# A hybrid attention block: the low part of the queries in zero-padded 128-row tiles

## The chip, the cores and the metric

The kernel runs on one core of one Trainium2 chip. The metric is device time in microseconds from start to end of one launch. TensorE (PE) multiplies, VectorE (DVE), ScalarE (ACT) and GpSimd (POOL) do the elementwise work, and SyncE (SP) issues the DMAs. A number like L413 is line 413 of the kernel before; the changed kernel's lines stand a few higher.

## The reference

One transformer block on 1024 tokens of width 1024, all in float32. A normalised input is projected into two attentions. The first (8 heads of 64) mixes three dilated windows, which is one softmax with a table of log multiplicities. The second (8 heads in 2 groups, one key head per group) has three branches: compressed keys, the 8 best blocks of 64 keys, and a window of 512. Their outputs are gated and summed, both attentions are normalised and projected, and a feed-forward layer with squared ReLU follows.

```python
s = jnp.einsum('bhrnqd,bhrnkd->bhrnqk', qs, kb) * (hd ** -0.5)      # dilated
sc = jnp.einsum('bgrqd,bgcd->bgrqc', qb, k_cmp) * scale             # compressed keys
p_cmp = masked_softmax(sc, cmp_end[None, :] <= tpos[:, None])
imp = jnp.einsum('bgrqc,cs->bgqs', p_cmp, overlap)                  # ranks the blocks
ss = jnp.einsum('bgrqd,bgqkd->bgrqk', qb, kg) * scale               # selected blocks
sw = jnp.einsum('bgrqd,bgkd->bgrqk', qb, kw) * scale                # window
out = gb[..., 0:1] * o_cmp + gb[..., 1:2] * o_sel + gb[..., 2:3] * o_win
h_res = h_res + mixed @ w_out[l]
h_res = h_res + jnp.square(jax.nn.relu(h @ w_up[l])) @ w_down[l]
```

## The kernel before

Float32 products are made from numbers split in two: a high part in the rounded format fp32r and a low part, the rest. A projection or MLP product is three matmuls: high x high, high x low, low x high (L334 to L336 for the projections, L709 to L711 for out_proj, L1021 to L1023 and L1055 to L1057 for the MLP).

Scores use that a head has only 64 rows. `k_stacks` and `q_stacks` turn 128-token tiles over on PE (L359) and stack two halves into 128 rows. For an even head (or group 0) the key stack holds the high keys in rows 0 to 63 and the low keys in rows 64 to 127; for an odd head (or group 1) it is the other way round. The query stack has the high queries in both halves. So one 128-row pass (L411) gives high x high + high x low. The low queries lie in a tile `q2`: rows 0 to 63 those of the even head, rows 64 to 127 those of the odd one. A second pass (L413) takes the 64 rows of the head and the same 64 rows of the key stack, which are its high keys, and adds low x high to the same bank. The queries are the stationary operand, up to 512 key columns the moving one. A unit is one head of one 128-query tile; more than 4 key blocks are cut in two chunks. Each chunk takes one of three score banks `S`.

The rest of a unit: DVE adds a table (window, multiplicity or block mask) and takes the extreme (L422), ACT exponentiates (L427), ACT, DVE and POOL split the result into two float16 parts (L441, L443, L445), a DMA on SP's queue transposes them into `pt` (L446), and PE multiplies them with the values (L461, L462). In the sparse attention the diagonal block of a selected branch gets its causal mask by a matmul with an identity (L415).

For the compressed keys of a 128-query tile (L754 to L758), each of four head pairs gets a 128-column pass of `q2` against `kch` (the high keys of group 0 and group 1, zeros elsewhere, so that all 128 rows of `q2` serve both groups), a mask by an identity matmul, and one 64-column pass per group of the query stack against `kcs`.

The stages in time: normalisation and the first projections to about 70 us; dilated attention of four head pairs between the other projections (scores from 71 to 337 us); the last projections; sparse attention over eight query tiles in the order 5, 7, 6, 4, 3, 2, 1, 0, between which out_proj is pushed in pieces (scores from 372 to 724 us); and the MLP from about 760 us to the end. The order on each engine is set by a scheduler in the compiler from priorities and its own cost model. The projections have a lower priority than the attention, so they fill in.

`cst`, `asp`, `bqp` and `bpp` are memory pools. `asp` lives through the dilated attention; `bqp` and `bpp` hold what the sparse attention needs, `bpp` from when the projection's memory is free. A query tile of the sparse attention is loaded from DRAM into `qr` (`q_load`, L734) and stacked (`q_build`) a tile ahead of its use. Names in the profile: `S`, `T`, `F`, `O` are banks (scores, transposes, products, outputs), `aq` and `ak` the stacks of the dilated attention, `qb` and `kb` those of the sparse one.

Of the kernel before, what the change touches and what calls it, by code (L numbers as in the profile page):

```python
# [9 lines left out]
F32 = mybir.dt.float32  # L10
# [27 lines left out]
FB = "qr qb qb2 ot cs cm oc".split()  # L38
# [7 lines left out]
CM = 1  # L46
# [10 lines left out]
def build(tc, A, out):  # L57
# [315 lines left out]
    def q_stacks(qe, qo, q2, srcs):  # L373
        n = len(srcs)
        ps = transposes(srcs)
        for e, o, i in zip(QS, (qe[0:64], qo[64:128], qe[64:128], qo[0:64]), (0, 64, 0, 64)):
            if e == "A":
                act.activation(o, ps[i:i + 64, :n], AF.Copy, scale=0.125)
            else:
                dve.tensor_scalar(o, ps[i:i + 64, :n], 0.125, None, op0=OP.mult)  # L380
        dve.scalar_tensor_tensor(q2[0:64], ps[0:64, :n], 0.125, f32(qe[0:64]), op0=OP.mult, op1=OP.subtract)
        dve.scalar_tensor_tensor(q2[64:128], ps[64:128, :n], 0.125, f32(qo[64:128]), op0=OP.mult, op1=OP.subtract)
# [11 lines left out]
    def st_scores(u):  # L394
# [12 lines left out]
        for j, (a, b) in enumerate(cuts):  # L407
# [5 lines left out]
            u["lastQ"] = pe.matmul(ps[:, :w], u["q2"], u["k"][u["r"], cs], start=False, stop=not diag)  # L413
# [107 lines left out]
    kch = cst.tile([128, 2, 64], F32R, name="kch")  # L521
    dve.tensor_scalar(kch, ident.rearrange("p (a b) -> p a b", a=2), 0.0, None, op0=OP.mult)
# [8 lines left out]
    def compress(kind):  # L531
# [36 lines left out]
        if kind == 0:  # L568
# [13 lines left out]
            act.activation(kch[0:64, 0], ps[0:64, 0, 0:64], AF.Copy)  # L582
            act.activation(kch[64:128, 1], ps[0:64, 0, 64:128], AF.Copy)
# [11 lines left out]
    def a_pair(hp):  # L595
# [5 lines left out]
        for a in (4, 0):  # L601
# [3 lines left out]
            q2 = asp.tile([128, 4, 128], F32R, name="aq2", bufs=1)  # L605
# [9 lines left out]
            for i in range(3, -1, -1):  # L615
                for e in range(2):
                    r = slice(64 * e, 64 * e + 64)
                    u = dict(q=q[:, e, i], q2=q2[r, i], r=r, k=k[:, e].rearrange("p a b -> p (a b)"),
# [7 lines left out]
    la = asp.tile([128, T], F32, name="la")  # L626
    sp.dma_start(la, A["la"])
# [102 lines left out]
    fbn = {}  # L730

    def q_load(i):
        QR[i] = big("qr0")[:, :512] if i == ORD[0] and "qr" in FB else bpp.tile([128, 512], F32, name="qr", bufs=2)
        sp.dma_start(QR[i], qbd[i])  # L734

    def q_build(i):
        q = fb(i, [128, 2, 4, 128], F32R, "qb", 2)
        q2 = fb(i, [128, 4, 128], F32R, "qb2", 2)
# [3 lines left out]

    def rows(g):
        return slice(64 * g, 64 * g + 64)

    def cmp_stages(i):
        st = {}

        def c1():
# [3 lines left out]
            for j in range(4):  # L753
                pe.matmul(ps[:, j], q2[:, j], kch, start=True, stop=False)  # L754
                if CM:
                    pe.matmul(ps[:, j], identb, cmask[:, i, None, :].to_broadcast([128, 2, 64]), start=False, stop=False)
                for g in range(2):
                    pe.matmul(ps[:, j, g], q[:, g, j], kcs[:, g], start=False, stop=g == 1)  # L758
# [48 lines left out]
    def b_attend(i, br):  # L807
# [4 lines left out]
        def f(br, h):  # L812
# [6 lines left out]
            u = dict(i=i, h=h, q=q[:, g, j], q2=q2[rows(g), j], r=rows(g), k=k[:, a * 128:], n=n,  # L819
# [53 lines left out]
    for step in P0:  # L873
        if step == "X":
# [14 lines left out]
            addt = bqp.tile([128, NT, 16], F32, name="addt")  # L889
            sp.dma_start(ctmp[:, :512], A["cmask"].rearrange("p a b -> p (a b)"))  # L890
# [35 lines left out]
    bpp, bpp_close = mkpool("bpp", side="right")  # L926
    for tag in ("ns", "hl", "pt"):
        xtra[tag] = (bpp, 0)
# [287 lines left out]
```

## Time and profile before

| what | value |
|---|---|
| time, median of 3 runs | 1474.64 us (1473.95 to 1474.69) |
| profiled execution, span | 1473.5 us |
| mean granted TensorE clock | 0.973 |
| PE, DVE, ACT, POOL busy | 98%, 55%, 42%, 35% |

The profiled execution shows its span from the first to the last instruction, 1473.5 us; the median run is 1.1 us above it. In a group of instructions stand the line, engine, operation, the tiles written and read, the sizes, the count, then the busy time in us and the mean of one in ns, then the idle time before them and what ended it. A matmul's size such as 64\*128 is rows and columns of its stationary tile. PE's busy time is modelled, and its matmuls overlap in the records: a matmul's record ends after the next has started, so the distance from start to start tells what one costs. In the tables by stretch PEclk is the granted clock as a share of full speed.

### The profile page before, as it was taken

Reading aid. Unit: us, or ns where it says so; the run is one execution under the profiler, and the core shown is the slowest. Engines: PE = TensorE matmul, PEld = TensorE weight load, DVE = VectorE, ACT = ScalarE, POOL = GpSimd, SP = SyncE. Lnnn points to the kernel's source line nnn. Section 1 sums busy time; section 2 is a strip of 40 time slices with the busy share of each in tenths; the row PEclk is TensorE's granted clock in tenths of the full one; section 3 lists DMA queues with packets and bytes.
Section 4 is the critical chain, followed back from the end, with each engine's and each line's share of the span. In section 5 each row is a group of like instructions: output and inputs, shape, how many; then the busy total and the mean of one; then the engine's idle time right before and its main releaser. Section 6 shows DMA issues by size and latency. Waiting matters only on the chain.

```text
span 1473.5 us, 21774 instructions
## 1 busy us (share of the span) xinstructions
PE 1437.5 (98%) x8235; PEld 1158.6 (79%) x8235; DVE 804.7 (55%) x1723; ACT 621.9 (42%) x1094; POOL 512.4 (35%) x728
## 2 busy tenths in 40 slices
PE   8999999999999999999899999999999999999997
PEld 6879888889866677677677888888888888888886
DVE  6565655774457776777545444444444444444436
ACT  7462746753656766677545221121221121221115
POOL 3435553654455556666711111111111111111113
PEclk9999999999968999799899999999999999999999
DMA  5255472957556866567523111111111111111002
GB/s 187 59 106 137 89 152 66 204 129 168 94 147 141 147 132 124 127 120 120 94 76 100 58 50 49 31 51 50 57 54 47 29 55 46 58 56 45 1 1 114
DMA packets 285192, 131.53 MB, mean 89 GB/s; under 512 B 219040, under 2 KB 272288, under 8 KB 285088
## 3 DMA queue, kind: packets, MB, share of 16 engines
q1 hardware_dynamic: 284944, 129.90, 37.8%
q8 instruction: 64, 1.05, 0.3%
q14 instruction: 40, 0.33, 0.1%
q10 hardware_dynamic: 144, 0.26, 0.0%
HBM read 68.26 MB, written 8.39 MB: 52 GB/s over the span
## 4 chain that ended last, share of the span: by engine, by line
PE 89%; DMA 3%; DVE 2%; POOL 2%; issue 1%; ACT 1%; SPq 0%; POOLq 0%; DVEq 0%; ACTq 0%
PE dn L1055 8%; PE dn L1057 8%; PE dn L1056 8%; PE up L1023 8%; PE up L1021 7%; PE up L1022 7%; PE S L413 7%; PE S L411 5%; PE F L334 4%; PE F L335 4%; PE F L336 4%; PE O L461 3%; PE T L359 2%; PE F L709 2%; PE F L710 2%; PE F L711 2%
## 5 line engine op out<-in xcount | busy, mean ns | idle before, releaser
L1032 POOL TENSOR_TENSOR ul<-ua,uh 128x512 fp32r<-128x512 f32 x64 | 83.5, 1305 | 611.0 <-ACT uh L1031 531.8
L1058 DVE SCALAR_TENSOR_TENSOR st<-dn,r2q,st 128x512 f32<-128x512 f32 (+1 forms) x257 | 191.5, 746 | 157.4 <-PE dn L1057 153.9
L1055 PE MATMUL dn<-wdh,uh 128*128 128x512 f32 (+1 forms) x514 | 202.8, 395 | 0.0
L1057 PE MATMUL dn<-wdh,ul 128*128 128x512 f32 (+1 forms) x514 | 202.3, 394 | 0.0
L1056 PE MATMUL dn<-wdl,uh 128*128 128x512 f32 (+1 forms) x514 | 201.4, 392 | 0.0
L1021 PE MATMUL up<-h2h,wuh 128*128 128x512 f32 x480 | 188.3, 392 | 1.0 <-ACT wuh L94 1.0
L1023 PE MATMUL up<-h2h,wul 128*128 128x512 f32 x480 | 188.4, 393 | 0.5 <-DVE wul L95 0.5
L1022 PE MATMUL up<-h2l,wuh 128*128 128x512 f32 x480 | 187.7, 391 | 0.0
L334 PE MATMUL F<-wh,hh 128*128 128x256 f32 (+1 forms) x576 | 166.5, 290 | 2.5 <-DVE vt L213 1.5
L335 PE MATMUL F<-wl,hh 128*128 128x256 f32 (+1 forms) x576 | 165.9, 289 | 0.0
L336 PE MATMUL F<-wh,hl 128*128 128x256 f32 (+1 forms) x576 | 164.5, 286 | 0.0
L427 ACT ACTIVATE ns<-ns,mn 128x640 f32<-128x640 f32 (+7 forms) x152 | 110.5, 747 | 58.1 <-POOL mn L426 28.8
L1029 ACT ACTIVATE ua<-up 128x512 f32<-128x512 f32 x60 | 35.3, 588 | 232.6 <-PE up L1023 232.6
L443 POOL TENSOR_TENSOR hl<-ns,hl 128x640 f16<-128x640 f32 (+5 forms) x67 | 104.0, 1554 | 36.3 <-ACT hl L441 30.4
L1057 PEld LDWEIGHTS dn<-wdh,ul 128*128 128x128 f32 x514 | 96.7, 188 | 22.6
L1056 PEld LDWEIGHTS dn<-wdl,uh 128*128 128x128 f32 x514 | 96.7, 188 | 21.9
L334 PEld LDWEIGHTS F<-wh,hh 128*128 128x128 f32 x576 | 108.1, 188 | 7.3 <-issue 3.4
L1055 PEld LDWEIGHTS dn<-wdh,uh 128*128 128x128 f32 x514 | 96.8, 188 | 21.1
L95 DVE TENSOR_TENSOR wul<-wur,wuh 128x1024 fp32r<-128x1024 f32 x32 | 39.4, 1230 | 134.4 <-ACT wuh L94 134.4
L335 PEld LDWEIGHTS F<-wl,hh 128*128 128x128 f32 x576 | 108.5, 188 | 4.5 <-issue 3.4
L336 PEld LDWEIGHTS F<-wh,hl 128*128 128x128 f32 x576 | 108.4, 188 | 3.7 <-issue 3.2
L1023 PEld LDWEIGHTS up<-h2h,wul 128*128 128x128 f32 x480 | 90.6, 189 | 20.5 <-DVE wul L95 1.0
(262 smaller groups left out, 3002.3 us busy)
## 6 DMA issues: line engine op xcount, KB each, us to landing
wur<-in_w_up_dram SPq DMA_DIRECT2D x32, 512.0 KB, 4.2
wdr<-in_w_down_dram SPq DMA_DIRECT2D x32, 512.0 KB, 3.8
wr<-in_w_in_dram SPq DMA_DIRECT2D x44, 256.0 KB, 3.2
st<-in_x_dram SPq DMA_DIRECT2D x8, 512.0 KB, 6.1
wor<-in_w_out_dram SPq DMA_DIRECT2D x16, 256.0 KB, 3.2
ns<-in_xT_dram SPq DMA_DIRECT2D x7, 512.0 KB, 4.9
out_dram<-st SPq DMA_DIRECT2D x7, 512.0 KB, 2.6
w<-in_w_k_dram SPq DMA_DIRECT2D x4, 512.0 KB, 5.1
```

The lines of the kernel that those rows point to most:

```text
L334: pe.matmul(ps, hh[:, k, ts], hi, start=k == 0, stop=False)
L335: pe.matmul(ps, hh[:, k, ts], lo, start=False, stop=False)
L336: pe.matmul(ps, hl[:, k, ts], hi, start=False, stop=k == KD - 1)
L427: u["exp"] = act.activation(ns[:, :n * 128], ns[:, :n * 128], AF.Exp, scale=-1.0, bias=mn[:, j:j + 1])
L443: pool.tensor_sub(lo, p, hi)
L1021: pe.matmul(ps, hi[:, k], h2h[:, k, hs], start=k == 0, stop=False)
L1022: pe.matmul(ps, hi[:, k], h2l[:, k, hs], start=False, stop=False)
L1023: pe.matmul(ps, lo[:, k], h2h[:, k, hs], start=False, stop=k == KD - 1)
L1055: pe.matmul(ps, uh[:, ts], wh[:, cs], start=j == 0, stop=False)
L1056: pe.matmul(ps, uh[:, ts], wl[:, cs], start=False, stop=False)
L1057: pe.matmul(ps, ul[:, ts], wh[:, cs], start=False, stop=j == NB - 1)
L1058: dve.scalar_tensor_tensor(o[:, cs], ps, r2q[:, t:t + 1], o[:, cs], op0=OP.mult, op1=OP.add)
```

## The change

The low queries move into a tile with a place of its own for each of the two heads (or groups). Head 0's low queries stand in rows 0 to 63 of the first half, and rows 64 to 127 there are zero; head 1's stand in rows 64 to 127 of the second half, and rows 0 to 63 there are zero. The second score pass then takes all 128 rows of this tile and all 128 rows of the key stack; the zeros meet the low keys. Three such tiles are made once and kept: `aq2` for the dilated attention, and two that take turns in the sparse one. Their zero halves are written once by DVE when the tile is made, two passes of 64 x 512 each.

The compressed keys use the same tiles: the pass against `kch` is replaced by one 64-column pass per group against `kcs`, the mask comes first, and `kch` with its zero fill and its two ACT copies is gone. The three tiles take twice the memory; `kch` and one of two `qr` buffers are given up.

```diff
-FB = "qr qb qb2 ot cs cm oc".split()
+FB = "qr qb ot cs cm oc".split()
...
-        dve.scalar_tensor_tensor(q2[0:64], ps[0:64, :n], 0.125, f32(qe[0:64]), op0=OP.mult, op1=OP.subtract)
-        dve.scalar_tensor_tensor(q2[64:128], ps[64:128, :n], 0.125, f32(qo[64:128]), op0=OP.mult, op1=OP.subtract)
+        dve.scalar_tensor_tensor(q2[0:64, 0], ps[0:64, :n], 0.125, f32(qe[0:64]), op0=OP.mult, op1=OP.subtract)
+        dve.scalar_tensor_tensor(q2[64:128, 1], ps[64:128, :n], 0.125, f32(qo[64:128]), op0=OP.mult, op1=OP.subtract)
+
+    def q2_tile(p, name):
+        t = p.tile([128, 2, 4, 128], F32R, name=name, bufs=1)
+        for e, rs in ((0, slice(64, 128)), (1, slice(0, 64))):
+            dve.tensor_scalar(t[rs, e], ident[rs, None, :].to_broadcast([64, 4, 128]), 0.0, None, op0=OP.mult)
+        return t
...
-            u["lastQ"] = pe.matmul(ps[:, :w], u["q2"], u["k"][u["r"], cs], start=False, stop=not diag)
+            u["lastQ"] = pe.matmul(ps[:, :w], u["q2"], u["k"][:, cs], start=False, stop=not diag)
...
-    kch = cst.tile([128, 2, 64], F32R, name="kch")
-    dve.tensor_scalar(kch, ident.rearrange("p (a b) -> p a b", a=2), 0.0, None, op0=OP.mult)
...
-            act.activation(kch[0:64, 0], ps[0:64, 0, 0:64], AF.Copy)
-            act.activation(kch[64:128, 1], ps[0:64, 0, 64:128], AF.Copy)
...
-            q2 = asp.tile([128, 4, 128], F32R, name="aq2", bufs=1)
+            q2 = aq2
...
-                    u = dict(q=q[:, e, i], q2=q2[r, i], r=r, k=k[:, e].rearrange("p a b -> p (a b)"),
+                    u = dict(q=q[:, e, i], q2=q2[:, e, i], k=k[:, e].rearrange("p a b -> p (a b)"),
...
+    aq2 = q2_tile(asp, "aq2")
...
-        QR[i] = big("qr0")[:, :512] if i == ORD[0] and "qr" in FB else bpp.tile([128, 512], F32, name="qr", bufs=2)
+        QR[i] = big("qr0")[:, :512] if i == ORD[0] and "qr" in FB else bpp.tile([128, 512], F32, name="qr", bufs=1)
...
-        q2 = fb(i, [128, 4, 128], F32R, "qb2", 2)
+        q2 = Q2[ORD.index(i) % 2]
...
-                pe.matmul(ps[:, j], q2[:, j], kch, start=True, stop=False)
-                if CM:
-                    pe.matmul(ps[:, j], identb, cmask[:, i, None, :].to_broadcast([128, 2, 64]), start=False, stop=False)
+                pe.matmul(ps[:, j], identb, cmask[:, i, None, :].to_broadcast([128, 2, 64]), start=True, stop=False)
                 for g in range(2):
+                    pe.matmul(ps[:, j, g], q2[:, g, j], kcs[:, g], start=False, stop=False)
                     pe.matmul(ps[:, j, g], q[:, g, j], kcs[:, g], start=False, stop=g == 1)
...
-            u = dict(i=i, h=h, q=q[:, g, j], q2=q2[rows(g), j], r=rows(g), k=k[:, a * 128:], n=n,
+            u = dict(i=i, h=h, q=q[:, g, j], q2=q2[:, g, j], k=k[:, a * 128:], n=n,
...
+            Q2.append(q2_tile(bqp, "qb20"))
...
+    Q2.append(q2_tile(bpp, "qb21"))
```

The scheduler orders the changed program anew. Up to the last head pair of the dilated attention it stands nearly as before; in the sparse stage pieces of out_proj and of the products with the values change places with scores. Three places matter for the prediction.

On PE, the scores against the compressed keys of the second query tile in the sparse attention. Before:

```order
L411 MATMUL S<-kb,qb 128x256
L413 MATMUL S<-kb,qb_5515 128x256
L754 MATMUL S<-kch,qb_5894 128x2x64
L756 LDWEIGHTS identb
L756 MATMUL S<-cmask,identb 128x2x64
L758 MATMUL S<-kcs,qb_5893 128x64 x2
```

Now:

```order
L417 MATMUL S<-kb,qb 128x256
L419 MATMUL S<-kb,qb_5449 128x256
L754 LDWEIGHTS identb
L754 MATMUL S<-cmask,identb 128x2x64
L756 MATMUL S<-kcs,qb_4806 128x64
L757 MATMUL S<-kcs,qb_5896 128x64
L756 MATMUL S<-kcs,qb_4806 128x64
L757 MATMUL S<-kcs,qb_5896 128x64
```

The score pair stands as it stood (the listing gives the size of the output, not the rows of the stationary tile). A 128-column pass is gone and two of 64 columns are new.

On DVE, where the key stack of the selected branch is built (L370, L371), at the start of the sparse stage. Before:

```order
L213 TENSOR_SCALAR st<-F,rms 128x128
L213 TENSOR_SCALAR vt<-F,r1v 128x128
L836 TENSOR_SCALAR den<-ot_4853,vsc 128x8
L837 RECIPROCAL den<-den 128x8
L370 TENSOR_TENSOR kb_5452<-T,kb_5452 64x512
```

Now:

```order
L213 TENSOR_SCALAR st<-F,rms 128x128
L213 TENSOR_SCALAR vt<-F,r1v 128x128
L387 TENSOR_SCALAR qb_5449<-c_ident 64x512 x2
L835 TENSOR_SCALAR den<-ot_4846,vsc 128x8
L836 RECIPROCAL den<-den 128x8
L370 TENSOR_TENSOR kb_5452<-T,kb_5452 64x512
```

The zero fill of the second sparse tile now stands three instructions ahead of that stack.

On SP's queue, the query loads. Before:

```order
L734 DMA qr<-qbd 128x512 x2
L682 DMA st<-in_x_dram 128x1024 x2
L734 DMA qr<-qbd 128x512
L656 DMA wor<-in_w_out_dram 128x512
L681 DMA oat<-oad 128x512
```

Now:

```order
L737 DMA qr<-qbd 128x512
L684 DMA st<-in_x_dram 128x1024 x2
L737 DMA qr<-qbd 128x512
L658 DMA wor<-in_w_out_dram 128x512
L683 DMA oat<-oad 128x512
```

The places are the same, and each holds the load of one tile earlier than before.

More of the change, by code (lines that the diff above doesn't have):

```diff
@@ L616, in a_pair @@
                 for e in range(2):
-                    r = slice(64 * e, 64 * e + 64)
-                    u = dict(q=q[:, e, i], q2=q2[r, i], r=r, k=k[:, e].rearrange("p a b -> p (a b)"),
+                    u = dict(q=q[:, e, i], q2=q2[:, e, i], k=k[:, e].rearrange("p a b -> p (a b)"),
                              n=a + i + 1, tab=la[:, (7 - a - i) * 128:],
@@ L730, in build @@
     fbn = {}
+    Q2 = []
     def q_load(i):
-        QR[i] = big("qr0")[:, :512] if i == ORD[0] and "qr" in FB else bpp.tile([128, 512], F32, name="qr", bufs=2)
+        QR[i] = big("qr0")[:, :512] if i == ORD[0] and "qr" in FB else bpp.tile([128, 512], F32, name="qr", bufs=1)
         sp.dma_start(QR[i], qbd[i])
@@ L741, in q_build @@
         QB[i] = (q, q2)
-    def rows(g):
-        return slice(64 * g, 64 * g + 64)
     def cmp_stages(i):
```

## The prediction

> **What bounds the kernel now.** First the busy rows and the chain of waits on the page.
>
> ```profile
> PE 1437.5 (98%) x8235; PEld 1158.6 (79%) x8235; DVE 804.7 (55%) x1723; ACT 621.9 (42%) x1094; POOL 512.4 (35%) x728
> ...
> PE 89%; DMA 3%; DVE 2%; POOL 2%; issue 1%; ACT 1%; SPq 0%; POOLq 0%; DVEq 0%; ACTq 0%
> PE dn L1055 8%; PE dn L1057 8%; PE dn L1056 8%; PE up L1023 8%; PE up L1021 7%; PE up L1022 7%; PE S L413 7%; PE S L411 5%; PE F L334 4%; PE F L335 4%; PE F L336 4%; PE O L461 3%; PE T L359 2%; PE F L709 2%; PE F L710 2%; PE F L711 2%
> ```
>
> TensorE is 89% of the chain. The two score passes stream the same columns, yet the low pass (L413) takes 7% and the high pass (L411) 5%. Next, busy time by stage: dilated attention beside projections (70 to 338 us), and sparse attention beside out_proj (372 to 724 us).
>
> ```profile
> core 0: us, PE busy (x) PEld busy (x) DVE busy (x) ACT busy (x) POOL busy (x), PEclk, DMA share, GB/s
> 70.00:338.00 268.00, 263.32 (x2066) 224.76 (x2065) 164.13 (x418) 151.95 (x290) 138.90 (x259) 1.00 0.58 125
> 372.00:438.00 66.00, 63.92 (x426) 51.45 (x424) 36.01 (x113) 37.38 (x78) 37.11 (x77) 0.85 0.52 123
> 438.00:724.00 286.00, 284.23 (x1929) 201.74 (x1928) 211.04 (x635) 194.32 (x335) 180.84 (x202) 0.93 0.68 126
> ```
>
> PE sets the pace in both. Elsewhere DVE has 61% of the first stage, but 247 us of the 352 of the second (36 + 211, 70%), where ACT has 232 and POOL 218. That is the room a faster PE has. Who waits for whom agrees: DVE waits for the low pass, and the queue of the transposes waits for PE to give back its buffers.
>
> ```profile
> DVE ns L422 <- PE S L413: 54.2, 57, 3.4
> ...
> SPq L446 <- PE O L462: 73.9, 36, 4.2
> ```
>
> **What a score pass costs.** The view of line 413 (ns: min/median/max) shows what the change does away with: stationary tiles of 64 rows.
>
> ```profile
> L413 PE MATMUL S<-kb,qb x192: 276/439/792, 374.0 to 724.0; 64*128 64x384 f32 x80, 64*128 64x256 f32 x56, 64*128 64x512 f32 x40, 64*128 64x128 f32 x16
> L413 PE MATMUL S<-ak,aq x96: 322/439/502, 72.7 to 336.7; 64*128 64x384 f32 x40, 64*128 64x512 f32 x32, 64*128 64x256 f32 x16, 64*128 64x128 f32 x8
> ```
>
> There are 288. Durations overlap, so the price is the distance between starts. The timeline of PE at full clock:
>
> ```profile
> 561.17 0.50 PE L413 MATMUL S<-kb,qb 64*128 64x512 f32 x1
> 561.60 0.45 PE L411 MATMUL S<-kb,qb 128*128 128x384 f32 x1
> 561.97 0.44 PE L413 MATMUL S<-kb,qb 64*128 64x384 f32 x1
> 562.34 0.23 PE L461 MATMUL O<-v,pt 128*128 128x129 f16 x1
> ...
> 564.27 0.39 PE L709 MATMUL F<-woh,mh 128*128 128x512 f32 x1
> 564.51 0.40 PE L710 MATMUL F<-wol,mh 128*128 128x512 f32 x1
> 564.74 0.39 PE L711 MATMUL F<-woh,ml 128*128 128x512 f32 x1
> 564.97 0.28 PE L411 MATMUL S<-kb,qb 128*128 128x256 f32 x1
> 565.18 0.38 PE L413 MATMUL S<-kb,qb 64*128 64x256 f32 x1
> 565.49 0.44 PE L411 MATMUL S<-kb,qb 128*128 128x384 f32 x1
> ```
>
> Full-row neighbours L709 to L711 start 0.233 us apart for 512 columns, 0.456 ns a column, with a different stationary tile each: the weight load is hidden. That makes 0.175 us for 384 columns and 0.117 for 256. L413 with 512 columns holds PE 0.43 us, L411 and L413 with 384 hold it 0.37 each, L413 with 256 holds it 0.31. Into a 64-row pass and out of it again, PE thus loses 0.19 to 0.20 us each (once here, at 564.97, only 0.09 on the way in). **Upper price:** 288 pairs x 2 x 0.19 = 109 us; with the smaller ones on the way in I take 105.
>
> The Trainium skill, TensorEngine Tiling (Array Packing), Key Properties, says that changing the tiling mode drains the engine; by that the loss ends once all passes have 128 rows. The trace agrees with its 0.19 us, and the sum is then the one below.
>
> **Lower price, from the chain.** Columns per pass: dilated 8 heads x 36 blocks x 128 = 36,864; sparse 8 x (36 + 30) x 128 = 67,584. At 0.456 ns both passes need 33.6 and 61.6 us. The chain over 60 to 340 us (280 us) and over 372 to 760 us (388 us):
>
> ```profile
> by line: PE F L334 15.7%; PE F L335 15.5%; PE F L336 15.1%; PE S L413 11.6%; PE S L411 7.6%; PE S L554 5.2%; PE O L461 4.7%; PE T L359 4.0%; PE O L462 2.3%; DMA wr<-in_w_in_dram 2.3%; POOL st L545 2.1%; issue 1.9%; DMA pt<-hl 1.9%; DMA w<-i
> ...
> by line: PE S L413 17.4%; PE S L411 12.4%; PE O L461 8.8%; PE F L709 8.5%; PE F L710 8.1%; PE F L711 7.9%; PE T L359 5.0%; PE O L462 4.1%; PE S L415 2.5%; PE F L334 2.5%; PE F L335 2.5%; PE O L782 2.4%; PE F L336 2.3%; issue 1.9%; PE S L758
> ```
>
> Dilated: 19.2% of 280 = 54, less 33.6 = 20 us. Sparse: 29.8% of 388 = 116, less 61.6 = 54 us. Some of the 54 is clock: the stage rows' clocks of 0.85 and 0.93 mean 20 + 40 = 60 us at half speed; with 30% of that in scores, 18 us, 9 of them are slow streaming. So 20 + 45 = 65 us lie on the chain at least. Taking all streaming as on the chain understates it.
>
> **Dilated stage.** Between 20 and 105/3 = 35 us; I take the middle, 28. Afterwards DVE has 164 of 240 us (68%), ACT 63%: they don't bind, and projections fill PE's waits.
>
> **Sparse stage.** PE alone gives between 45 and 70 us, middle 58, leaving 294 us, in which DVE would be busy 84%. Its best stretch of 40 us is
>
> ```profile
> 440.00:480.00 40.00, 39.03 (x250) 27.46 (x249) 30.45 (x89) 25.95 (x45) 23.31 (x25) 0.80 0.68 137
> ```
>
> or 76%. Held to that, 247 us take 325, a gain of 27. It is no ceiling, since PE was the brake, but new waits begin there: the score bank is freed by DVE's pass (L422) and L411 queues behind it on PE with everything after it. Between 27 and 58 I take 43.
>
> **Compressed keys.** Each of 32 query blocks loses the zero-padded 128-column pass (L754) and gains two of 64 columns.
>
> ```profile
> 468.35 0.33 PE L754 MATMUL S<-kch,qb 128*128 128x128 f32 x1
> 468.51 0.23 PE L756 MATMUL S<-cmask,identb 128*128 128x128 bf16 x1
> 468.56 0.39 PE L758 MATMUL S<-kcs,qb 128*128 128x64 f32 x2
> 468.78 0.31 PE L754 MATMUL S<-kch,qb 128*128 128x128 f32 x1
> ```
>
> L754 holds PE 0.16 us, two L758 hold it 0.22: +0.06 x 32 = +2 us, with PE's path.
>
> **Zero fills.** Six DVE passes of 64 x 512, two per tile. Nearest rows:
>
> ```profile
> L522 DVE TENSOR_SCALAR kch<-c_ident 128x128 fp32r<-128x128 f32 x1 | 0.2, 220 | 0.0
> L667 DVE TENSOR_SCALAR wor<-wor,gvec 128x512 f32<-128x512 f32 x16 | 11.5, 721 | 0.1
> ```
>
> Between 0.22 and 0.72 us each; 0.7 as it has the same length. The pair for the dilated tile and that of the first sparse tile lie under projection matmuls. The third stands ahead of the keys of the selected branch, for which PE waits today:
>
> ```profile
> PE S L411 <- DVE kb L370: 1.2, 1, 1.2
> ```
>
> Up to 1.4 us late there, partly in idle DVE time: +1. Without the cover all six cost 4.2. The removed key fill (0.22) and two small ACT copies are off the path: 0.
>
> **Query load.** One buffer fewer. The load of a tile now waits for the transposes of the tile before it, which run a tile earlier than it is needed (the sparse stage's 352 us over 8 tiles: 44 us, against 3.5 us to land):
>
> ```profile
> qr<-qbd SPq DMA_DIRECT2D x8, 256.0 KB, 3.5
> ```
>
> It keeps its places among the transposes on SP's queue: 0. If a load stood in that queue for a late tile, its 3.5 us would hold back the transposes behind it, once a tile.
>
> **Sum**, against the profiled span 1473.5: -28 - 43 + 2 + 1 = -68, so 1405.5; the median run stands 1.1 above the span: **1406.6 us**.
>
> **Rivals.**
>
> *The softmax engines take over the sparse stage.* DVE stays at 76% (gain 27), and a PE that waits more falls into half clock once more. Rows of such a stretch, entered after a PE stall of under 1 us:
>
> ```profile
> 600.00:605.00 5.00, 4.31 (x26) 2.64 (x25) 4.93 (x18) 2.52 (x5) 2.92 (x4) 1.00 0.89 182
> 605.00:610.00 5.00, 5.00 (x31) 3.45 (x30) 5.00 (x15) 3.98 (x6) 4.81 (x4) 0.58 0.69 169
> 610.00:615.00 5.00, 5.00 (x20) 2.89 (x19) 4.93 (x15) 2.27 (x4) 4.71 (x5) 0.50 0.70 132
> 615.00:620.00 5.00, 5.00 (x18) 2.80 (x19) 2.83 (x9) 3.81 (x6) 2.78 (x4) 0.50 0.35 66
> ```
>
> Some 20 us at half speed lose 10. Then -28 - 27 + 10 + 3 = -42: 1433. For it: DVE is full in these rows already. Against: its 54 us of waiting for L413.
>
> *All of it is realised.* -105 + 3: 1373. Against: 247 us of DVE in 282 would be 88%.
>
> *The clock gives it all back: slower.* Where PE runs ahead of DVE, each wait may halve its clock. At full clock PE's sparse work is 352 - 30 - 58 = 264 us; with the whole stage at half, twice that, 528, is 176 more than 352: 1474.6 - 28 + 176 = 1623. It decides from 232 us at half speed on (264 + 116 = 352 + 28). Today there are 60; against it also that half speed makes PE late again and ends its waits.
>
> *The drain isn't one of row modes.* Then the 0.19 us belong to a load that stays exposed, and only the costs remain: 1474.6 + 3 = 1477.6. For it: the loss is as long as a weight load. Against: L709 to L711 load full tiles at no cost. The Trainium skill, TensorE: Matmul & The Clock Gate, Part 3, "What overlaps and what doesn't", says that a weight load overlaps a running matmul only where the row groups differ; full-row passes would then expose every load. The 0.233 us of L709 to L711 contradict it here.
>
> **Chances.** The forecast 0.66, the softmax engines 0.17, all realised 0.08, no drain 0.05, slower 0.04. A change under 0.2% (3 us) can't be told from none. So faster 0.91, same 0.05, slower 0.04. The range runs from all realised, 1370, to the softmax engines with some more waiting, 1440.
>
> **What would show it.** Right: L419 has the form 128*128; starts of L417 to L419 lie 0.23 us apart for 512 columns and 0.18 for 384; the chain's score lines fall to about 33 + 62 us; dilated stage some 28 us shorter, sparse some 43; the L756 and L757 pairs 0.2 us; MLP unchanged. PE should now wait for DVE (L428) in the sparse stage. Wrong: score passes still 0.37 us for 384 columns (no drain), PE idle over 40 us there (softmax engines), or a clock under 0.8 in that stage (slower).

## The result, and the profile after

The changed kernel takes 1435.51 us (median of four runs, 1430.88 to 1436.64). The kernel before, run beside it, took 1474.3 us (1472.52 to 1474.69). The ratio is 0.973, with an interval of 0.971 to 0.975. The gain is 39 us, where 68 were forecast. The profiled span is 1434.6 us at a mean clock of 0.976.

The page of the changed kernel: busy rows, chain by engine, chain by line.

```profile
PE 1356.6 (95%) x8267; PEld 1150.8 (80%) x8267; DVE 804.2 (56%) x1728; ACT 620.4 (43%) x1092; POOL 512.7 (36%) x728
...
PE 65%; POOL 7%; DVE 7%; DMA 7%; issue 4%; ACT 4%; SPq 0%; POOLq 0%; DVEq 0%; ACTq 0%
PE dn L1056 8%; PE dn L1058 8%; PE dn L1057 8%; PE up L1024 8%; PE up L1022 8%; PE up L1023 8%; DMA pt<-hl 2%; PE F L334 2%; PE F L335 2%; PE F L336 2%; PE T L359 1%; DVE ns L428 1%; PE S L417 1%; POOL hl L449 1%; DMA pt<-hlx 1%
```

PE's share of the chain falls from 89% to 65%. The two score lines, 12% of the chain before, leave one entry of 1%. In their place stand the links of a unit's own loop: DVE's pass over a score bank (L428, before L422), POOL's split (L449), the transpose (`pt<-hl`).

The second score pass is now L419 (the first is L417). The view of that line shows the new form in both stages:

```profile
L419 PE MATMUL S<-kb,qb x192: 273/338/615, 358.2 to 686.1; 128*128 128x384 f32 x80, 128*128 128x256 f32 x56, 128*128 128x512 f32 x40, 128*128 128x128 f32 x16
L419 PE MATMUL S<-ak,aq x96: 273/338/775, 71.7 to 317.4; 128*128 128x384 f32 x40, 128*128 128x512 f32 x32, 128*128 128x256 f32 x16, 128*128 128x128 f32 x8
```

The last dilated pass starts at 317.4 us (before 336.7), the last sparse one at 686.1 (before 724.0). PE's timeline, at full clock, shows what a pass costs now:

```profile
507.66 0.19 PE L468 MATMUL O<-v,pt 128*128 128x65 f16 x1
507.69 0.42 PE L417 MATMUL S<-kb,qb 128*128 128x384 f32 x1
507.95 0.34 PE L419 MATMUL S<-kb,qb 128*128 128x384 f32 x1
508.12 0.28 PE L417 MATMUL S<-kb,qb 128*128 128x256 f32 x1
508.24 0.28 PE L419 MATMUL S<-kb,qb 128*128 128x256 f32 x1
508.61 0.50 PE L417 MATMUL S<-kb,qb 128*128 128x512 f32 x1
508.95 0.40 PE L419 MATMUL S<-kb,qb 128*128 128x512 f32 x1
509.20 0.23 PE L467 MATMUL O<-v,pt 128*128 128x129 f16 x1
```

L419 holds PE 0.17 us for 384 columns and 0.25 for 512, where the pass before held it 0.37 and 0.43: the 0.19 us behind it are gone. The pass of 256 columns at 508.24 stands 0.37 us ahead of the next start, 0.25 more than its streaming; the row behind it names no cause. Such pauses are counted as score time in the table below.

**PE's time, stage by stage.** From PE's timeline each matmul is charged the distance to the next start, less the idle time that the rows show. Stage A runs from 60 us to the first sparse score; stage B from there to the first down-projection of the MLP. The column of the compressed keys holds their scores, their mask and the product with their values.

| us | A: length | scores high / low | projections | idle | B: length | scores high / low | compressed keys | out_proj | idle |
|---|---|---|---|---|---|---|---|---|---|
| before | 312.5 | 28.5 / 34.6 | 193.0 | 6.0 | 418.6 | 67.2 / 74.7 | 23.6 | 101.2 | 10.7 |
| after | 296.8 | 20.2 / 19.6 | 188.0 | 18.4 | 395.5 | 45.6 / 40.0 | 26.6 | 98.6 | 40.0 |

The scores cost 79.6 us less (23.3 in A, 56.3 in B). Idle time is 41.7 us more (12.4 and 29.3), the compressed keys 3.0 more, all else 3.9 less: together 38.8 less, the gain. **The change removed more from PE than was forecast to reach the end, and over half of it turned into waiting.** The MLP behind it is as long as before; its first down-projections start at these times (of before, then of after), 682 us ahead of the end in both:

```profile
L1055 PE MATMUL dn<-wdh,uh x514: 279/394/398, 791.1 to 1463.6; 128*128 128x512 f32 x170, 128*128 128x256 f32 x2
```

```profile
L1056 PE MATMUL dn<-wdh,uh x514: 279/395/398, 752.3 to 1424.7; 128*128 128x512 f32 x170, 128*128 128x256 f32 x2
```

What PE waits for, over the span (waiting line, cause, us in total, times, longest). Before:

```profile
PE O L461 <- DMA pt<-hl: 2.0, 2, 1.2
PE S L411 <- DVE mn L422: 1.7, 3, 1.0
```

After, with DVE's wait for PE:

```profile
DVE ns L428 <- PE S L419: 23.3, 29, 2.1
PE O L467 <- DMA pt<-hl: 19.4, 22, 2.9
PE S L417 <- DVE mn L428: 12.1, 14, 2.3
PE O L467 <- DVE dena L479: 5.6, 3, 3.3
PE O L467 <- DMA pt<-hlx: 5.0, 5, 2.0
```

DVE's wait for PE has more than halved (from 54.2). PE now waits for DVE to free a score bank, as forecast (12.1 us), and for transposed probabilities, twice as much (19.4 + 5.0), which was not forecast.

The sparse stage of the changed kernel by stretch (us, busy time of PE, PEld, DVE, ACT, POOL, granted clock, DMA share, GB/s), the second row its middle part, the third DVE's best stretch before:

```profile
360.00:680.00 320.00, 287.54 (x2327) 239.22 (x2327) 244.31 (x728) 226.40 (x399) 209.79 (x268) 0.94 0.72 136
420.00:690.00 270.00, 240.05 (x1974) 195.17 (x1973) 216.68 (x644) 198.31 (x346) 186.84 (x214) 0.96 0.76 140
440.00:480.00 40.00, 36.85 (x292) 29.64 (x292) 34.91 (x112) 28.39 (x44) 22.44 (x24) 0.95 0.75 145
```

DVE is busy 76% of the stage, the share at which the rival of the softmax engines held it; but over 440 to 480 us it reaches 87%. (Not all of this is DVE's own work: see experiments 5 and 6.)

### The profile page after: what moved, and what is told of

The parts are those of the page before. It is cut to its first block, busy times and chain, and to the rows that moved or that the text cites. A ratio compares the mean times of both kernels' runs of the same rounds, so it can differ in the third digit from the quotient of the medians.

```text
span 1434.6 us, 21829 instructions
## 1 busy us (share of the span) xinstructions
PE 1356.6 (95%) x8267; PEld 1150.8 (80%) x8267; DVE 804.2 (56%) x1728; ACT 620.4 (43%) x1092; POOL 512.7 (36%) x728
## 4 chain that ended last, share of the span: by engine, by line
PE 65%; POOL 7%; DVE 7%; DMA 7%; issue 4%; ACT 4%; SPq 0%; POOLq 0%; DVEq 0%; ACTq 0%
PE dn L1056 8%; PE dn L1058 8%; PE dn L1057 8%; PE up L1024 8%; PE up L1022 8%; PE up L1023 8%; DMA pt<-hl 2%; PE F L334 2%; PE F L335 2%; PE F L336 2%; PE T L359 1%; DVE ns L428 1%; PE S L417 1%; POOL hl L449 1%; DMA pt<-hlx 1%
## 5 line engine op out<-in xcount | busy, mean ns | idle before, releaser
L467 PE MATMUL O<-v,pt 128*128 128x129 f16 x816 | 93.6, 227 | 30.0 <-DMA pt<-hl 19.4
L449 POOL TENSOR_TENSOR hl<-ns,hl 128x640 f16<-128x640 f32 (+5 forms) x67 | 104.4, 1560 | 27.5 <-ACT hl L447 21.6
L467 PEld LDWEIGHTS <-pt 128*128 128x128 f16 x816 | 74.1, 100 | 48.8 <-DMA pt<-hl 26.7
```

Of the source, the lines that this page charges most:

```text
L449: pool.tensor_sub(lo, p, hi)
L467: pe.matmul(ps, ph, v[:, 0:129], start=t == 0, stop=False)
```

## The experiments

Each kernel is compared with the kernel before, run beside it on the same chip (1475.29, 1474.79 and 1474.44 us in the three groups of runs). In the diffs, lines with - are those of the changed kernel unless said otherwise.

**1 and 2. One stage at a time.** The first kernel has the zero-padded tile in the dilated attention alone; the sparse one keeps its 64-row tile, `kch` and both `qr` buffers. Against the changed kernel:

```diff
-        q2 = Q2[ORD.index(i) % 2]
+        q2 = fb(i, [128, 4, 128], F32R, "qb2", 2)
...
-            u = dict(i=i, h=h, q=q[:, g, j], q2=q2[:, g, j], k=k[:, a * 128:], n=n,
+            u = dict(i=i, h=h, q=q[:, g, j], q2=q2[rows(g), j], r=rows(g), k=k[:, a * 128:], n=n,
```

> The 128-row tile only in the dilated attention; sparse attention and compressed keys as before. Theory (the loss sits at each change between 64-row and 128-row passes, and part of it comes back as waits in the same stage): the dilated stage shortens by the 19 us seen in the changed kernel (last dilated score at 317 instead of 336 us), the sparse stage keeps its 352 us: about 1455 us. Rival (the two stages hand their delays on, so that one alone gives little): under 10 us, over 1465. If the no-drain rival were right: 1474.

Measured: 1475.67 us (1466.93 to 1479.29, ten runs), ratio 1.000 (0.998 to 1.002): no gain. The mixed forms show that the edit did what it says. The view of its second pass:

```profile
L421 PE MATMUL S<-kb,qb x192: 276/439/792, 361.3 to 728.2; 64*128 64x384 f32 x80, 64*128 64x256 f32 x56, 64*128 64x512 f32 x40, 64*128 64x128 f32 x16
L421 PE MATMUL S<-ak,aq x96: 274/338/774, 72.3 to 319.9; 128*128 128x384 f32 x40, 128*128 128x512 f32 x32, 128*128 128x256 f32 x16, 128*128 128x128 f32 x8
```

The last dilated score starts 17 us earlier than before (319.9 against 336.7), the first sparse second pass 13 us earlier (361.3 against 374.0), and the last one 4 us later (728.2 against 724.0): all is given back in stage B.

The second kernel has it in the sparse attention alone; the compressed keys as in the changed kernel.

```diff
-            u["lastQ"] = pe.matmul(ps[:, :w], u["q2"], u["k"][:, cs], start=False, stop=not diag)
+            u["lastQ"] = pe.matmul(ps[:, :w], u["q2"], u["k"][u["r"], cs], start=False, stop=not diag)
...
-            q2 = aq2
+            q2 = asp.tile([128, 4, 128], F32R, name="aq2", bufs=1)
```

> The 128-row tiles only in the sparse attention and the compressed keys; dilated attention as before. Theory: the sparse stage shortens by the 22 us seen in the changed kernel, the dilated stage stays: about 1452 us, and the two gains add up to that of the whole change. Rival (stages hand on delays): the two single gains miss the 39 us of the whole by over 8 us.

Measured: 1451.86 us (1447.66 to 1452.98), ratio 0.984 (0.982 to 0.987): a gain of 23.

| us | A: length | idle | B: length | scores | projections | out_proj | idle | clock loss in B |
|---|---|---|---|---|---|---|---|---|
| before | 312.5 | 6.0 | 418.6 | 141.9 | 27.1 | 101.2 | 10.7 | 35.9 |
| dilated only | 299.8 | 18.2 | 433.0 | 144.0 | 30.3 | 104.8 | 16.9 | 40.1 |
| sparse only | 314.9 | 8.2 | 393.5 | 82.8 | 26.8 | 101.4 | 41.5 | 25.6 |
| both | 296.8 | 18.4 | 395.5 | 85.6 | 30.9 | 98.6 | 40.0 | 22.2 |

(Clock loss is the sum over stretches of 5 us, from 340 to 800 us, of the time by one less the granted clock. It overlaps the other columns. Each row is one execution. Those of the kernel before and of the changed kernel have the lowest granted clock of their runs: 0.973, where 27 others show 0.974 to 0.982, and 0.976, where three others show 0.978 to 0.982.)

What follows: the gains don't add. Alone they are 0 and 23 us, together 39. The 1455 us expected of the first kernel failed and its rival held; the 1452 of the second came true. The dilated part shortens A by 12.7 us added to the kernel before (312.5 to 299.8) and by 18.1 added to the sparse one (314.9 to 296.8), and this survives only where the sparse stage has full-row passes too. In the kernel with the dilated part alone B grows by 14.4 us: mainly 3.2 of left-over projections, 6.2 of waiting, 3.6 of out_proj and 2.1 of scores, the last two in a stage with 4.2 us more clock loss. Not the profiled execution alone is low in clock: the first kernel's ten runs have a median of 0.966, the thirteen of the kernel before 0.979. Over the span that is some 19 us more clock loss, about what the dilated part wins in A. Whether the clock takes the gain back, and whether this is an effect of 64-row passes or of the order that the scheduler chose there, these two kernels don't tell.

**3. Less PE work in the sparse stage.** The changed kernel without the low pass of the compressed keys (their product with the low queries is left out):

```diff
                 for g in range(2):
-                    pe.matmul(ps[:, j, g], q2[:, g, j], kcs[:, g], start=False, stop=False)
                     pe.matmul(ps[:, j, g], q[:, g, j], kcs[:, g], start=False, stop=g == 1)
```

> The changed kernel without the 64 low passes of the compressed keys (L756): the product of the low queries with the compressed keys is left out. PE loses 64 passes that hold it 8.4 us. Theory (PE waits in the sparse stage now, so what is taken from PE there is worth about half): 3 to 5 us less than the changed kernel, about 1431. Rival (PE still bounds): 8 us less, 1427. Rival (PE no longer matters there): the same, 1435.

Measured: 1435.11 us (1429.79 to 1438.67), ratio 0.973 (0.970 to 0.976), that of the changed kernel. PE's time for the compressed keys falls from 26.6 to 20.2 us; B stays at 395.1 (395.5), its idle time 41.6. **Six microseconds less of PE work make no difference that these runs can show.** Two limits: the interval is some 5 us wide either way, and the profiled execution has 10 us more clock loss from 340 to 800 us (32.4 against 22.2). The 3 us which the compressed keys cost more than before are then likely off the path too.

**4. Half the transposes.** The changed kernel transposes the high part of the probabilities alone, and the product that takes the low part takes the high part again (the low part is left out of the result; the work of PE stays).

```diff
-        sp.dma_start_transpose(pt[:, :2 * n], hl[:, :2 * w])
+        sp.dma_start_transpose(pt[:, :n], hl[:, :w])
...
-            x["pt"] = [(pt[:, m + t], pt[:, n + m + t]) for t in range(x["n"])]
+            x["pt"] = [(pt[:, m + t], pt[:, m + t]) for t in range(x["n"])]
```

> The changed kernel with half of each transposing DMA: only the high part of the probabilities is transposed, and the product with the values' low... second pass takes the high part again, so the low part of the probabilities is left out of the result; the work on PE, DVE, ACT and POOL stays. Theory A (what is lost comes back as PE waiting for the transposes, because these DMAs are slow or crowded): the waits of L467 for pt, 24 us, go and the kernel falls by 15 to 30 us, to 1405 to 1420. Theory B (the transposes are late because their inputs are late: DVE and the chain behind it): under 8 us, 1428 or more.

Measured: 1426.63 us (1425.38 to 1427.87), ratio 0.968 (0.966 to 0.970), 9 us below the changed kernel, between what the two theories had. All of it comes from stage A (285.8 us against 296.8); B is 395.4. The stretch of its sparse stage that answers to the one above:

```profile
420.00:690.00 270.00, 239.68 (x1930) 196.52 (x1928) 205.35 (x634) 193.24 (x344) 187.19 (x217) 0.93 0.40 80
```

The DMA engines are busy 40% instead of 76%, and the stage is as long: the transposes' width does not set it, though PE waits for them. In the dilated stage it costs 11 us: PE's idle time there falls from 18.4 to 14.1 us, and the clock loss over 0 to 340 us from 8.5 to 1.7.

**5 and 6. More work for DVE.** A pass of 128 x 320 over a tile of its own, once for each transposed unit of the sparse stage, into the kernel before and into the changed one:

```diff
+    dum = []
...
     def st_trans(us):
         u = us[0]
+        if dum:
+            dve.tensor_scalar(dum[0], dum[0], 1.0, None, op0=OP.mult)
...
+    dum.append(bpp.tile([128, 320], F32, name="dum"))
+    dve.memset(dum[0], 1.0)
```

> The kernel before with an idle DVE pass of 128 x 320 added for each of the 82 transposed units of the sparse stage after its first branch: by the rows of 0.22 us for 128 and 0.72 for 512 columns some 0.45 us each, 37 us of DVE. All theories: PE bounds this kernel, DVE has 100 us to spare in the stage; up to 10 us slower, under 1485.

> The same 82 DVE passes in the changed kernel. Theory D (the sparse stage is now limited by how much DVE has to do): over 20 us slower, 1455 or more. Theory L (it is limited by the length of the chain from score to transposed probabilities and by the order on PE, not by the amount of work on DVE): under 12 us slower, below 1448.

Measured: 1509.86 us for the kernel before with it (1508.8 to 1511.27; ratio 1.024, 1.022 to 1.025), +35 us. And 1450.62 for the changed kernel with it (1448.95 to 1456.19; ratio 0.984, 0.982 to 0.987), +15. For the kernel before at most 10 were expected, for the changed one under 12 or over 20. The load itself is nearly the same in both. First the one before (ns: min/median/max, first and last start):

```profile
L434 DVE TENSOR_SCALAR dum<-dum x88: 308/324/2226, 418.7 to 559.6; 128x320 f32<-128x320 f32 x88
```

Then the changed one:

```profile
L440 DVE TENSOR_SCALAR dum<-dum x88: 307/322/1949, 402.4 to 540.3; 128x320 f32<-128x320 f32 x88
```

It is 54 us of DVE time in the changed kernel (52 in the one before), bunched in 139 us because these passes wait for no input. The same stretch of the changed kernel, first without the load, then with it:

```profile
402.00:541.00 139.00, 121.84 (x997) 97.16 (x996) 112.44 (x318) 103.89 (x164) 90.30 (x101) 0.96 0.81 163
```

```profile
402.00:541.00 139.00, 111.18 (x811) 88.87 (x812) 136.21 (x357) 88.30 (x137) 77.63 (x80) 0.88 0.69 145
```

With the load DVE is busy 98% of that stretch (136 of 139 us), without it 81%. So the changed kernel's DVE is not busy all the time without it: 54 us more lengthen the kernel by 15. But 15 isn't nothing either. **How long DVE is busy is one part of what sets the stage, not all of it.**

And busy is not all work. Rows of DVE and POOL, in order of time, in the changed kernel with the load:

```profile
490.99 0.32 DVE L440 TENSOR_SCALAR dum<-dum 128x320 f32<-128x320 f32 x1
491.45 2.15 POOL L453 TENSOR_TENSOR hlx<-nsx,hlx 128x1024 f16<-128x1024 f32 x1
491.83 1.95 DVE L440 TENSOR_SCALAR dum<-dum 128x320 f32<-128x320 f32 x1
```

The second of these DVE passes starts inside a POOL pass and ends 0.18 us after it. So do all 27 that took over 0.5 us: each ends 0.18 to 0.19 us after a POOL pass that ran when it started. 88 passes at the median of 0.32 us would be 28 us; the rest of the 54 is DVE waiting for POOL inside its recorded time. DVE's own part of the split shows the same in the changed kernel without the load: of its 14 passes of 640 columns in the sparse stage nine take 0.80 to 0.83 us, one 0.97, and the four that start well inside a long POOL pass 1.32 to 2.00. Set against the median of its form where no POOL pass runs, some 30 of DVE's 244 us over 360 to 680 us are such waiting (an estimate).

In the kernel before, where DVE has the larger slack, the same load cost more than twice as much; B grows by 34 us, PE's idle time there by 9.5, and the clock loss from 35.9 to 63.2. A stretch of that kernel:

```profile
420.00:475.00 55.00, 52.38 (x199) 34.38 (x200) 47.28 (x116) 31.05 (x50) 27.76 (x28) 0.53 0.62 155
```

PE is recorded as nearly always busy, at half speed: 27 us more clock loss stand against a loss of 35. The clocks of all runs agree: 0.955 to 0.959 in four with the load, 0.978 to 0.980 in the seven without it beside them, some 36 us more clock loss over the span. With DVE work added to both kernels, the change is worth 59 us instead of 39.

**7 and 12. The split moved between POOL and DVE.** A table of three letters says which engine forms the low part of the probabilities: DVE or POOL. The first kernel gives all three to POOL, the second two to DVE.

```diff
-LOB = "DPP"
+LOB = "PPP"
```

> The changed kernel with the low parts of all probabilities of the sparse stage on POOL (a third of them was on DVE): DVE loses 31 passes of 1.06 us, 33 us; POOL gains 31 of 1.55 us, 48 us, and comes to about 265 of 330 us. Theory D: 10 to 20 us faster, 1415 to 1425. Theory L: no faster, since the POOL pass is longer and POOL is nearly as full: 1435 to 1450.

Measured: 1454.49 us (1449.57 to 1455.96), ratio 0.985 (0.983 to 0.988), +19 on the changed kernel; B 413.0, idle 49.6. Moving this work from DVE to POOL makes it slower; over the span DVE is busy 19 us less and POOL 47 us more (785.0 and 559.8), so the run doesn't test DVE alone.

```diff
-LOB = "DPP"
+LOB = "DDP"
```

> The changed kernel with two thirds of the low parts of the sparse stage's probabilities on DVE in place of one third: POOL loses some 30 passes of 1.56 us (47 us), DVE gains 30 of 1.06 us (32 us) and comes to about 280 of 330 us. Theory D: 10 us slower or more. Theory P (POOL's longer passes are what makes the chain long, since more of them cost 19 us): 5 to 15 us faster, 1420 to 1430.

Measured: 1440.1 us (1435.43 to 1445.68), ratio 0.977 (0.974 to 0.981), some 5 us above the changed kernel; the intervals overlap. Its sparse stage:

```profile
360.00:680.00 320.00, 290.36 (x2272) 246.38 (x2271) 252.19 (x718) 220.34 (x381) 155.33 (x196) 0.90 0.68 134
```

POOL is busy 155 us instead of 210, DVE 252 instead of 244 (over the span 53 less and 17 more), and nothing is gained; either theory had expected 5 us or more to one side. The profiled execution is the slowest of the four (1445.7), at the lowest clock. POOL's amount of work by itself isn't the bound either.

**8. PE in the order of the program.** The changed kernel with PE's order in the sparse stage as the program issues it, instead of the scheduler's:

```diff
-    ms = tc.manual_schedule(engines={eng[x] for x in ""}) if "" else ExitStack()
+    ms = tc.manual_schedule(engines={eng[x] for x in "P"})
```

> The changed kernel with PE's instructions of the sparse stage in the order in which the program writes them (products with the values three units behind their scores, out_proj pieces and compressed keys at the places where they are pushed) in place of the order that the scheduler makes. Theory O (the scheduler's order asks for transposed probabilities too early, which costs PE its 40 us of idle time): the waits of L467 for pt fall under 10 us and the kernel gains 10 us or more, under 1425. Theories D and L: no gain, 1433 or more, since the inputs are late whatever the order.

Measured: 1515.17 us (1509.19 to 1521.05), ratio 1.027 (1.024 to 1.030): 80 us slower. PE's waits from 345 to 800 us:

```profile
PE O L467 <- DMA pt<-hl: 41.4, 20, 4.7
PE O L467 <- DMA pt<-hlx: 27.5, 11, 5.9
```

B is 476.8 us with 99.6 idle, most of it PE standing before the transposes of the unit that comes next in the order. So theory O, a gain of 10 us or more, fails; the others' 'no gain' holds, though none foresaw a loss of this size. The program's order is no remedy; that some third order waits less isn't excluded.

**9 to 11. Units in flight, and buffers.** The number of units between score and value product in the sparse stage is 3. The first kernel has 2; the second a fourth buffer for transposed probabilities, paid with one of two buffers of the output tiles and that of the transposed compressed scores, which take the place of the scores; the third that and 4 units.

```diff
-DEPA, DEPB = (1, 3)
+DEPA, DEPB = (1, 2)
```

> The changed kernel with the products with the values of the sparse stage written two units behind their scores in place of three. Theory L (the time from a score to its transposed probabilities, against the number of units in flight, sets the sparse stage): 15 us slower or more, 1450 or above, with more waiting of PE for pt. Theory D (amount of work on the softmax engines): within 5 us of 1435.

```diff
-        pt = alt("pt", [128, 16, 128], FH, 0)
+        pt = alt("pt", [128, 16, 128], FH, 1)
...
-        OA[i] = bpp.tile([128, 512], F32, name="oat", bufs=2)
+        OA[i] = bpp.tile([128, 512], F32, name="oat", bufs=1)
```

> The changed kernel with a fourth buffer for the transposed probabilities in the sparse stage; its memory comes from the transposed compressed scores, which take the place of the scores themselves, and from one of the two buffers of the dilated output's loads. Theory L: one more unit in flight, PE's 40 us of idle time in the sparse stage fall by a quarter or more: 1420 to 1428. Theory D: no change beyond 3 us.

```diff
-DEPA, DEPB = (1, 3)
+DEPA, DEPB = (1, 4)
...
-        pt = alt("pt", [128, 16, 128], FH, 0)
+        pt = alt("pt", [128, 16, 128], FH, 1)
```

> The kernel with four pt buffers, and the products with the values four units behind the scores. Theory L: 8 us or more under the changed kernel, below 1427. Theory D: as the changed kernel, 1432 to 1438.

Measured: 1432.91 (1429.91 to 1438.49; ratio 0.973, 0.970 to 0.976), 1438.4 (1434.7 to 1441.89; 0.976, 0.973 to 0.980) and 1437.52 us (1430.07 to 1438.47; 0.974, 0.971 to 0.978). B is 390.5, 397.9 and 394.9 us, with 42.5, 48.4 and 40.0 idle. None can be told from the changed kernel: the depth is not the bound, nor are the buffers of `pt`, unless what was given up for the fourth cost as much as it gained. No run with the whole arithmetic measurably beats the changed kernel.

## Why the prediction came out as it did

**That changing between 64-row and 128-row passes costs PE time: right.** The pass that was not edited got cheaper with the one that was. L411/L417 fell from 95.7 to 65.8 us over both stages, L413/L419 from 109.3 to 59.6. The two kernels with one part each show it stage by stage: the scores got cheaper only where the passes have 128 rows. The rival without a drain is out. The Trainium skill, TensorEngine Tiling (Array Packing), Key Properties, says that a mode switch needs a drain; these starts agree. The Trainium skill, TensorE: Matmul & The Clock Gate, Part 3, "What overlaps and what doesn't", has a weight load overlap a running matmul only where the row groups differ; the 0.17 us of L419 for 384 columns, with a stationary tile of its own each time, speak against that.

**Its size: the upper price was too high.** Forecast were 105 us of PE time (288 pairs, 0.19 us twice with a little less on the way in), measured 79.6, between the two prices of 65 and 105. The sparse term on PE alone was right (58 forecast, 56.3 measured), the dilated one smaller (28, 23.3). The step that failed is "(once here, at 564.97, only 0.09 on the way in)" and the 105 us taken from it. Sorted by what stands ahead of a pair, over pairs with no wait beside them (medians, us beyond 0.456 ns a column):

| ahead of the pair | before: pairs, first pass, second pass | after: pairs, first pass, second pass |
|---|---|---|
| a second pass | 67, 0.198, 0.197 | 58, 0.002, 0.005 |
| a full-row matmul of 256 columns or more | 87, 0.093, 0.195 | 72, 0.001, 0.001 |
| a matmul of 162 columns or fewer | 108, 0.177, 0.195 | 106, 0.085, 0.004 |

The 0.09 was the rule for 87 of 262 pairs, not the exception. And behind a short matmul (108 pairs) 0.085 us of the first pass belong to no switch: they stay. A pair gained 0.28 to 0.29 us in these two classes and 0.39 only behind another pair. (These medians make it 0.31 us a pair, 90 over 288; the ledger's 79.6 counts all pairs, and the unexplained pauses beside them as score time.)

**Dilated stage: "projections fill PE's waits" failed.** PE lost 23.3 us of scores there and waits 12.4 us more, so that A is 15.7 shorter, where 28 was forecast and 20 the lower bound. DVE and ACT were no bound, as the text said, but nothing covered the single waits. PE's largest after the change, from 60 to 320 us:

```profile
PE O L467 <- DMA pt<-hl: 4.1, 5, 1.5
PE O L467 <- DVE dena L479: 2.2, 2, 1.8
PE F L334 <- ACT wh L94: 2.2, 2, 1.1
PE S L417 <- DVE mn L428: 1.8, 3, 1.2
```

They are many and small, and no one of them takes the place of the drain. Halving the transposes gave 11 us back there, part of it as clock. That the clock loss ahead of 340 us rose from 1.7 to 8.5 us with the change was not forecast either; the ten kernels with the dilated part and whole transposes have 5 to 10 us there, the three without the part 2 to 3.

**Sparse stage: the working was right on PE and wrong on what is realised.** 56.3 us left PE and 29.3 came back as waiting, 3.0 as compressed keys. B is 23.1 shorter, where 43 - 3 was forecast and the lower bound was 27 - 3 = 24. The text named the test itself, PE idle over 40 us; the stage has 40.0, the edge of it. The time, 1435.5, lies 2 us from the rival's 1433, but that rival is borne out in part only. For it: DVE at 76%, and the new wait at L417. Against it: DVE can be busy 98% of a stretch of this stage (part of it waiting for POOL), freeing POOL or adding DVE work moves the time by a fraction, moving work from DVE to POOL makes it slower, and its 10 us of a new half-clock stretch didn't come. From 340 us on the clock loss fell from 35.9 to 22.2 us in the two profiled executions (over the first 800 us together from 37.6 to 30.7); over all runs the mean clocks are alike, a median of 0.979 before and 0.976 to 0.982 after. The rival's sum was close because its dilated term was 12 too favourable and its clock term 10 too dear. The middle between bounds, 43, had no row behind it; the lower bound, from DVE's best 40 us, had one.

**What bounds the sparse stage now is left open.** It stayed at 390 to 398 us with 6 us less PE work, with DMA at half its share, with 2 or 4 units in flight and with 4 `pt` buffers. It grew by a part of the time added to DVE, and by 17.5 us with the low part moved to POOL (with it moved to DVE by 7, but in the slowest of four executions). PE still holds 355 of its 395 us. No resource taken alone was shown to set it; that each unit's loop over several engines does, with PE too full to cover every wait, would fit all of these, but was not shown. One part of such a loop was left untested: DVE's passes that wait for POOL's (experiments 5 and 6). No run keeps the two apart, and none keeps the order of the kernel before under full-row passes.

**The small terms.** Compressed keys +3.0 on PE, without an effect on the end that experiment 3 could show. The forecast of +2 was for their scores and mask alone, which cost 4.0 more (14.3 to 18.3 us); the product with the values cost 1.1 less. Rows of PE's timeline for a head pair there:

```profile
446.80 0.23 PE L754 MATMUL S<-cmask,identb 128*128 128x128 bf16 x1
446.84 0.28 PE L756 MATMUL S<-kcs,qb 128*128 128x64 f32 x1
446.95 0.28 PE L757 MATMUL S<-kcs,qb 128*128 128x64 f32 x1
447.06 0.28 PE L756 MATMUL S<-kcs,qb 128*128 128x64 f32 x1
447.17 0.28 PE L757 MATMUL S<-kcs,qb 128*128 128x64 f32 x1
```

A pair of L756 and L757 takes 0.22 us (forecast 0.2). The zero fills take 0.42 to 0.50 us, inside their bounds of 0.22 and 0.72; the query loads and the MLP cost nothing, as forecast. That all would be realised (1373) and that the clock would give it back (1623) both failed. Of the signs named for being right, one came out otherwise: the chain's score lines were to fall to 33 + 62 us, and they fell to 15 us (60 to 340 us) and 19 (stage B), since the chain now runs through the waits.

## What to carry to other kernels

Where two kinds of pass alternate, measure starts against a neighbour of the same kind, sorted by what stands ahead; padding a half-height stationary tile with zeros cost no streaming time, and took 0.28 to 0.39 us off a pair. Of 56 us taken from the busiest engine of a stage, where the next ran at 70%, 23 were realised, though no other engine was busy all the time: take the row-backed lower bound, not the middle. Look at how long the passes of one form take before reading a busy share as work: part of it can be waiting for another engine. A gain in one stage can vanish in the next; try the parts alone before adding their gains.

## What the hardware showed that had not been expected

**Half speed that lasts while PE is recorded busy.** Two stretches of the kernel before (PE's busy time is the third number, the granted clock the third from the end):

```profile
420.00:445.00 25.00, 25.00 (x89) 16.03 (x90) 14.72 (x42) 14.54 (x23) 13.29 (x14) 0.50 0.70 191
605.00:625.00 20.00, 20.00 (x92) 12.55 (x92) 14.34 (x40) 13.15 (x21) 14.48 (x14) 0.52 0.44 93
```

In the kernel with the change in the dilated attention alone, whose sparse passes have 64 rows, the same:

```profile
410.00:435.00 25.00, 24.80 (x87) 15.26 (x88) 15.03 (x41) 15.38 (x25) 14.59 (x14) 0.52 0.69 191
```

And three of the changed kernel, the first its longest unbroken one:

```profile
372.50:382.70 10.20, 10.20 (x60) 10.01 (x61) 4.99 (x18) 5.68 (x13) 4.96 (x10) 0.50 0.83 120
450.00:460.00 10.00, 7.83 (x58) 6.32 (x57) 7.58 (x24) 7.70 (x15) 6.80 (x10) 0.83 0.53 119
570.00:595.00 25.00, 18.37 (x129) 13.92 (x128) 20.55 (x54) 17.66 (x30) 20.03 (x21) 0.80 0.70 148
```

With 64-row passes in the sparse stage (three kernels) the clock is at half for up to 24, 27 and 51 us at a time, although PE is recorded as busy nearly throughout. The few matmuls that start there fit it: 89 in 25 us, where the changed kernel starts 997 in 139. The first row of the changed kernel shows that full-row passes don't rule this out, but there it lasted 10 us. In the eleven kernels with full-row passes the half-speed stretches of this stage are 3 to 14 us, except for one of 17 in the kernel with the order of the program and one of 21 with the low part on POOL, which both had PE idle for part of them. These stages have 38 to 50 us of waiting (99.6 in the order of the program) instead of 11 to 20, and their clock loss is 17 to 38 us (66.8) where the three others have 36, 40 and 63. That the full-row stage loses less clock on the whole is not firm: the 36 us of the kernel before come from its execution with the lowest clock (0.973 against a median of 0.979, some 9 us over the span). Whether the 64 rows, the drains inside the recorded time or something else keep the clock down isn't separated by these runs. The Trainium skill, TensorE: Matmul & The Clock Gate, Part 1, "What's actually happening", has the full clock back after one busy window of about 3.4 us; time recorded as busy was not enough for it here.

**A matmul behind a short one.** In the changed kernel a first score pass behind a matmul of 162 columns or fewer holds PE 0.08 to 0.11 us beyond its streaming at full clock, whatever its own length and whether the short one is float16, bfloat16 or float32; behind 256 columns or more it is 0.006 us or less in the median. The rows at 507.69 (behind L468, 0.26 us to the next for 384 columns) and 508.12 (behind L419, 0.12 for 256) show both.

**A DVE pass that waits inside its recorded time.** The rows of experiments 5 and 6 show it: a pass of 0.32 us is recorded with up to 1.95 when it starts while POOL is in a pass, and all 27 over 0.5 us end 0.18 to 0.19 us after that POOL pass (so do all 25 in the kernel before, up to 2.23). Not every kind of DVE pass is held: the passes over the score banks (L428) of 384 columns have the same median inside and outside POOL's long passes, 0.55 to 0.56 us.
